# A diffusion trunk's modulation vectors: matmuls with thin weights replaced by row sums on VectorE

## Chip, core and metric

One core of a Trainium2 chip runs the whole program: two layers over 256 context and 256 latent tokens. The metric is device microseconds (us) of one execution; the profile is one further execution.

## What is computed

Each layer derives six modulation vectors of 1024 features from a conditioning vector, once for the latent stream (`c`) and once for the context stream (`c_ctx`):

```python
mod_x = jnp.split((jax.nn.silu(c) @ w_mod[layer] + b_mod[layer])[:, None, :], 6, axis=-1)
mod_c = jnp.split(jax.nn.silu(c_ctx) @ w_mod[layer] + b_mod[layer], 6, axis=-1)
hx = modulate(rms_norm(x, norm_pre_mix[layer]), mod_x[0], mod_x[1])       # shift, scale
x = x + mod_x[2] * rms_norm(mix_x, norm_post_mix[layer])                  # gate
hx = modulate(rms_norm(x, norm_pre_ffn[layer]), mod_x[3], mod_x[4])
x = x + mod_x[5] * rms_norm(channel_mixer(hx), norm_post_ffn[layer])
```

`w_mod[layer]` is 1024 by 6144, 24 MB in f32. The rest of a layer is a token mixer (mLSTM, HGRN2 and differential attention side by side) and a channel mixer: dense SwiGLU in the first layer, top-2 of 8 experts in the second. The second layer's context stream is only needed for its mixer's inputs, so of its modulation the context needs the first two sixths alone.

## The kernel before

Large products are f32 matmuls in three passes: each weight tile of 128x1024 is split into a high part (`whi`, ScalarE, `whl` line 188) and a low part (`wlo`, a VectorE subtraction), and `mm3` (line 196) issues three matmuls per block. Pairs of `whi` and `wlo` live in a ring: three in the pool `wp`, and two more in the pool `hr` during the first half of the dense part. Weights arrive as 1 MB loads by `load` (line 164) in a ring of raw slots, four in `wp` and four more in `hr`; SyncE (SP) issues them all.

The stages follow each other: mixer 0, dense (gate and up, then down), mixer 1, experts. The modulation is computed in pieces spread over them. `first_mods` makes the first two sixths of layer 0 at the very start. All else goes through `mod_piece(l, g, n)` (line 236): a third `g` of `w_mod[l]` (2048 columns) and two of its eight row blocks (`n`), by two 1 MB loads; for each row block four matmuls into the four 32-column strips of the array, with silu(c) as weights (tile `pm`), and an addition into `macc`; after the fourth piece four transposes (`mt`), the bias, and `mod_affine` (line 314), which multiplies by the norm weights into `aff`.

These pieces are generators in a list `work`, and so are projections of the mixers (`fm`, `tm`). `tick(n)` (line 291) advances the list by n units between the steps of a stage, and it starts the first two entries, which issues their loads. Layer 0's last two thirds (`mods(0, 1) + mods(0, 2)`) stand in mixer 0 between projections. Layer 1's twelve pieces (`mo1`, line 1373) stand: two in mixer 0's attention (line 1299), one in the tail of mixer 0 (line 1342), three in the dense part (line 1394), and six in mixer 1 (line 960). In the gate-and-up loop (lines 1391 to 1405) one `tick(1)` follows each of 40 groups; a group is one `whl` and 24 matmuls into the tile `pgu`, and two groups end in one `swiglu_out` (line 1384), a VectorE product into `hh`.

A planner of the framework puts every instruction in an order per engine before the run, from its own model of durations. Only where `strict` is set (mixer 1's end, experts) is program order kept. `row_out` (line 325) writes a feature vector as 4-byte elements to a DRAM tile `gd`, and `row_in` (line 335) reads it back as a row on all 128 partitions.

Of the kernel before, what the change touches and what calls it, by code (L numbers as in the profile page):

```python
# [12 lines left out]
F32 = mybir.dt.float32  # L13
F32R = mybir.dt.float32r
BF16 = mybir.dt.bfloat16
# [3 lines left out]
ALU = mybir.AluOpType  # L19
AX = mybir.AxisListType  # L20

P = 128
D = 1024
# [32 lines left out]
V_L = 16  # L56
V_PM, V_QM, V_PF, V_QF, V_BM, V_GB, V_LB, V_MN, V_HN, V_DN = 0, 8, 16, 24, 32, 80, 81, 85, 87, 89
V_LN = 90
# [51 lines left out]
def kernel(ctx: ExitStack, tc: tile.TileContext, t: dict, out: bass.AP):  # L110
    nc = tc.nc
# [11 lines left out]
    MM, TR = ordered(nc.tensor.matmul), ordered(nc.tensor.transpose)  # L123
    ACT = ordered(nc.scalar.activation)
    TT, TS = ordered(nc.vector.tensor_tensor), ordered(nc.vector.tensor_scalar)
    STT, RED = ordered(nc.vector.scalar_tensor_tensor), ordered(nc.vector.tensor_reduce)
# [7 lines left out]
    sv = cp.tile([P, V_END], F32, name="sv")  # L134
# [7 lines left out]
    modT = [cp.tile([P, 48, 2], F32, name=f"modT{l}") for l in range(2)]  # L142
    aff = [cp.tile([P, 4, KT, 2], F32, name=f"aff{l}") for l in range(2)]
    sc = cp.tile([P, KT, 32], F32, name="sc")
# [4 lines left out]
    def bank(name, dt=F32):  # L149
        return psp.tile([P, 512], dt, tag="b", bufs=8, name=name)  # L150
# [13 lines left out]
    def load(ap, n=2048, halves=False):  # L164
        pool, b = pick("raw", (wp, 4))
        w = pool.tile([P, n], F32, tag="raw", bufs=b, name="raw")
        if halves:
            for a in (slice(0, n // 2), slice(n // 2, n)):
                nc.sync.dma_start(w[:, a], ap[:, a])
        else:  # L170
            nc.sync.dma_start(w[:, :n], ap)
        return w
# [60 lines left out]

    macc = cp.tile([P, 512], F32, name="macc")

    def mod_piece(l, g, n):

        ws = [load(t["w_mod"][l, k * P:(k + 1) * P, g * 2048:(g + 1) * 2048]) for k in (2 * n, 2 * n + 1)]
        yield
        pm = bank("pm")  # L240
        for k in (2 * n, 2 * n + 1):
            for q in range(4):
                MM(pm[32 * q:32 * q + 32, :], sc[:, k, :], ws[k % 2][:, q * 512:(q + 1) * 512],
                   start=(k % 2 == 0), stop=(k % 2 == 1), skip_group_check=True)
            yield
        if n == 0:
            nc.vector.tensor_copy(macc, pm)
            return
        TT(macc, pm, macc, op=ALU.add)
        if n < 3:  # L250
            return
        yield
        pt = bank("mt")
        for b in range(4):
            nc.tensor.transpose(pt[:, b * P:(b + 1) * P], macc[:, b * P:(b + 1) * P], ident)
        q = 16 * g
        b = sv[:, V_L + l * V_LN + V_BM + q:V_L + l * V_LN + V_BM + q + 16].rearrange("p (g b) -> p g b", g=4)
        TT(modT[l][:, q:q + 16, :].rearrange("p (g b) s -> p g b s", g=4),
           pt.rearrange("p (b g s) -> p g b s", b=4, g=4)[:, :, :, 0:2],
           b.unsqueeze(3).to_broadcast([P, 4, 4, 2]), op=ALU.add)  # L260
        for which in ((0,), (1,), (2, 3))[g]:
            mod_affine(l, which)

    def first_mods(c):

# [38 lines left out]
    def add(*gens):  # L304
        work.extend([g, False] for g in gens)
# [2 lines left out]
        while work:  # L308
            tick(1)

    def mods(l, g):
        return [mod_piece(l, g, n) for n in range(4)]

    def mod_affine(l, which):

        j, v = ((1, V_PM), (2, V_QM), (4, V_PF), (5, V_QF))[which]
        src = modT[l][:, 8 * j:8 * j + 8, :]
        v += V_L + l * V_LN
        n = sv[:, v:v + 8].unsqueeze(2).to_broadcast([P, 8, 2])
        if which in (0, 2):  # L320
            STT(aff[l][:, which], src, 1.0, n, op0=ALU.add, op1=ALU.mult)
        else:
            TT(aff[l][:, which], src, n, op=ALU.mult)

    def row_out(src, streams):

# [179 lines left out]
    def mixer(l, X, banks=None):  # L506
# [450 lines left out]
            ACT(mk_[:, j, :], pp, AF.Copy, scale=0.125)  # L957

        lag[0] = 1
        mo = mods(0, 1) + mods(0, 2) if l == 0 else mo1[6:]  # L960
        for g in (fm(None, 1, (0, 512), use_gt), fm(3, 2, (q0, 512), use_mq), fm(4, 2, (0, 512), use_mk)):
            add(g, *mo[0:1])
            mo = mo[1:]
# [61 lines left out]
        for g in ([fm(9 + c, 2, (q0, 512), use_o(2 * c)) for c in range(2)]  # L1025
# [3 lines left out]
            mo = mo[1:]  # L1029
# [25 lines left out]
        for dst, src in ((bT, g0), (thr, g2)):  # L1055
            pt = bank("pt")[:, 0:256].rearrange("p (a b) -> p a b", a=4)
# [7 lines left out]
        for h in range(4):  # L1064
            if h % 2 == 0:

                S = [hx.tile([P, 4, 512], F32, tag=tg, name="S") for tg in ("b8b", "b8c")]
                for s in range(4):
                    a, b = st_rng[s]
# [42 lines left out]
            for d in range(2):  # L1112
# [7 lines left out]
                dst = hs_[:, tr, h * 64:(h + 1) * 64]  # L1120
# [47 lines left out]
        op = ow.enter_context(tc.tile_pool(name=f"ow{l}", bufs=1))  # L1168
# [18 lines left out]
        if l:  # L1187
            first_raws.extend(load(EARLY[n]) for n in range(2))
            g = load_row(gd)
# [105 lines left out]
                    add(out_first(x[1]))  # L1295

        add(*mo)
        if not l:
            add(*mo1[:2])
        qs = {qt[0]: queries(qt[0])}  # L1300
        for tt in qt:
            if tt < 3:
# [19 lines left out]
        with tc.tile_pool(name=f"xw{l}", bufs=1) as xw, tc.tile_pool(name=f"xo{l}", bufs=1) as xo:  # L1322
            more.update(hl=[(xw, 6 if l == 0 else 2)], nhl=0)
            if l == 0:
                xr = {}
                for i in qt:
                    xr[i] = xo.tile([P, D], F32, tag="xr", bufs=4, name="xr")
                    nc.sync.dma_start(xr[i], t["xin"][i * P:(i + 1) * P, :])
                g = gate_in(xo, *gd, nc.sync)
            w_o = [whl(raw_o[n // 2][:, n % 2 * 1024:(n % 2 + 1) * 1024]) for n in range(4)]  # L1330
            py = {}

            def product(i):
                py[i] = bank("py")
                for _ in out_product(i, py[i]):
                    pass

            def post(*tiles):
                return post_steps(xo, [((mix[:, i, 0:512], py[i]), xr[i], g[:, 1 if i < 2 else 0, :], X[:, i, :]) for i in tiles])

            if l == 0:
                add(*mo1[2:3])
            if l == 0:
                with tc.tile_pool(name=f"xp{l}", bufs=1) as pn:
                    banks = tail(product, post, pn, X, (0, 2), 4, 8, lambda: Start((t["w_fg"][0], t["w_fu"][0])))
                more.update(hl=[], nhl=0)
                return banks
            product(2)
            product(3)
            strict[0] = True  # L1350
            steps = [post_steps(xo, [((mix[:, i, 0:512], py[i]), xr[i], g[:, 0, :], X[:, i, :])], i - 1) for i in qt]
            two, three = steps
            f2, f3 = ex.features(2), ex.features(3)
            for _ in two:
                pass
            for _ in range(4):
                next(three)
            next(f2)
            for _ in three:
                pass  # L1360
            next(f2)
            ex.square(2)
            ex.weighed(2, C2)
            ex.scale(2)
            next(f3)
            next(f3)
            ex.square(3)
            ex.weighed(3, C3)
            strict[0] = False
            return ex  # L1370


    mo1 = [g for n in range(3) for g in mods(1, n)]

    def dense(X, banks):
        with ExitStack() as es:
            hp = es.enter_context(tc.tile_pool(name="hp", bufs=1))
# [2 lines left out]
            hh = [slots(F32, f"hh{f}") for f in range(NF)]  # L1380
            with tc.tile_pool(name="hr", bufs=1) as hr:
                more.update(raw=[(hr, 4)], nraw=0, hl=[(hr, 2)], nhl=0)

                def swiglu_out(f, pg, pu):
                    sg = hr.tile([P, 512], F32, tag="sg", bufs=2, name="sg")
                    ACT(sg, pg, AF.Silu)
                    TT(hh[f], pu, sg, op=ALU.mult)

                for j in range(2):
                    swiglu_out(j, banks[j], banks[2 + j])  # L1390
                for c in range(1, NF // 2):
                    wg, wu = load(t["w_fg"][c]), load(t["w_fu"][c])
                    if c == 1:
                        add(*mo1[3:6])
                    for j in range(2):
                        ps = []
                        for w in (wg, wu):
                            a, b = whl(w[:, j * 1024:(j + 1) * 1024])
                            pd = bank("pgu")
                            for k in range(KT):  # L1400
                                kc = slice(k * P, (k + 1) * P)
                                mm3(pd, a[:, kc], b[:, kc], TH[:, k, :], TL[:, k, :], k == 0, k == KT - 1)
                            ps.append(pd)
                            tick(1)
                        swiglu_out(2 * c + j, *ps)
                drain()
# [3 lines left out]
            acc = [[bank("pd") for _ in range(2)] for i in range(4)]  # L1410
# [30 lines left out]
                for i in tiles[0:2 * (tiles[0] // 2)]:  # L1441
                    nc.sync.dma_start(xs[i * P:(i + 1) * P, :], X[:, i, :])

            add(*mo1[6:6])
            with tc.tile_pool(name="xpd", bufs=1) as pn:
                banks = tail(product, post, pn, X, (1, 0), 6, 8,
                             lambda: Start((t["w_fm"][1, 0], t["w_fm"][1, 1]), lambda: slots(F32R, "w_s")))
# [427 lines left out]
def pack(x, c, ctx, c_ctx, w_mod, b_mod, norm_pre_mix, norm_post_mix, norm_pre_ffn, norm_post_ffn,  # L1875
# [37 lines left out]
    rows[0, R_RB:R_RB + 8] = np.asarray(router_b)[0]  # L1913
    d["vecs"], d["rows"] = vecs, rows
    d["w_fm"], d["w_tm"], d["w_gt"] = np.stack(fm), np.stack(tm), np.stack(gt)
    d["w_mod"] = w_mod
    a = w_mod[0].reshape(2, 4, P, 6, 4, 256)[:, :, :, 0:2]
    d["w_m0"] = np.ascontiguousarray(a.transpose(4, 0, 2, 1, 3, 5).reshape(4, 2, P, 2048))
    d["w_out"] = np.stack([_tm(w_out[l]) for l in range(2)])
# [21 lines left out]
```

## Time and profile before

| what | us |
|---|---|
| median of 3 runs | 2217.36 (2217.22 to 2218.29) |
| profiled execution | 2215.78 |
| its span, first to last instruction | 2214.0 |
| mixer 0 | 0 to 499 |
| dense, gate and up | 499 to 733 |
| dense, down, and its tail | 733 to 880 |
| mixer 1 | 880 to 1185 |
| experts | 1185 to 2214 |

PE is TensorE's matmuls, PEld its weight loads, DVE VectorE, ACT ScalarE, POOL GpSimdE, SP the queue that issues the DMAs. A busy PE is not PE at its peak, since matmuls overlap in the records. A row in brackets with an arrow says how long an engine was idle before the instruction and which engine or DMA ended the wait.

### The profile page before, as it was taken

The page shows a single profiled execution, that of the slowest core. Times are in us where ns is not written, and L with a number is a line of the kernel's source. Part 1 is how long each engine was busy: PE and PEld are TensorE (multiplying, and loading weights), DVE is VectorE, ACT ScalarE, POOL GpSimd, SP SyncE. Part 2 cuts the span into 40 slices and gives each one's busy share as a digit, 9 for nine tenths or more (in the row PEclk, how much of TensorE's full clock was granted, in tenths as well). Part 3 has the DMA queues.
Part 4 walks back from the last instruction along what each step waited for, and adds up shares of the span by engine and source line. Part 5 has one row for each costly group of instructions (what it writes and reads, how often), then busy time and mean ns, then how long its engine had stood idle before and what let it go on. Part 6 is the DMA issues. An engine that isn't in the chain of part 4 may idle for free.

```text
span 2214.0 us, 27692 instructions
## 1 busy us (share of the span) xinstructions
PE 2118.2 (96%) x10532; PEld 1680.6 (76%) x10532; DVE 1566.6 (71%) x2145; ACT 1249.5 (56%) x1832; POOL 87.7 (4%) x82
## 2 busy tenths in 40 slices
PE   7998998999999999999987999999999999999997
PEld 4877666787888788777866888877777777777775
DVE  4758657773222346756678998888888888798887
ACT  3632445652222335524557777767777677776765
POOL 1000003010000001000111000000000000000000
PEclk9999999899999999999998999999999999999999
DMA  7430434047221331435437999899998999989992
GB/s 298 151 105 37 134 141 160 5 190 285 77 77 50 123 117 39 171 107 191 76 130 296 371 369 354 305 345 357 347 357 315 357 359 347 350 324 353 355 356 94
DMA packets 81357, 496.82 MB, mean 224 GB/s; under 512 B 17728, under 2 KB 18752, under 8 KB 23104
## 3 DMA queue, kind: packets, MB, share of 16 engines
q1 hardware_dynamic: 81216, 494.97, 60.7%
q8 instruction: 85, 1.39, 0.3%
q14 instruction: 56, 0.46, 0.1%
HBM read 492.81 MB, written 2.13 MB: 224 GB/s over the span
## 4 chain that ended last, share of the span: by engine, by line
PE 32%; DVE 10%; DMA 4%; issue 2%; ACT 2%; DVEq 0%; ACTq 0%
PE pg L117 19%; PE py L117 10%; DVE wlo L117 8%; DMA raw<-w_eu 3%; ACT whi L117 1%; DMA raw<-w_ed 1%; PE ph L1712 1%; PE pcb L117 0%; PE px L117 0%; DVE X L117 0%; DVE qh L1227 0%; DVE mx L1242 0%; DMA X<-w_eu 0%; PE po L117 0%; PE psc L117 0%
## 5 line engine op out<-in xcount | busy, mean ns | idle before, releaser
L117 DVE TENSOR_TENSOR wlo<-raw,whi 128x1024 fp32r<-128x1024 f32 x815 | 959.2, 1224 | 191.8 <-ACT whi L117 179.0
L117 ACT ACTIVATE whi<-raw 128x1024 fp32r<-128x1024 f32 (+1 forms) x820 | 815.4, 1055 | 273.5 <-PE pgu L117 148.8
L117 PE MATMUL pg<-wlo,TH 128*128 128x512 f32 x896 | 363.3, 405 | 5.7 <-DVE wlo L117 2.1
L117 PE MATMUL pg<-whi,TH 128*128 128x512 f32 x896 | 355.6, 397 | 0.8 <-DVE cf L117 0.8
L117 PE MATMUL pg<-whi,TL 128*128 128x512 f32 x896 | 352.1, 393 | 0.0
L117 PE MATMUL py<-whi,hhl 128*128 128x512 f32 x896 | 289.2, 394 | 0.0
L117 PEld LDWEIGHTS pg<-wlo,TH 128*128 128x128 f32 x896 | 168.3, 188 | 63.8 <-DVE wlo L117 30.2
L117 PEld LDWEIGHTS pg<-whi,TH 128*128 128x128 f32 x896 | 168.3, 188 | 40.3 <-DVE cf L117 1.3
L117 PEld LDWEIGHTS py<-whi,hhl 128*128 128x128 f32 x896 | 168.2, 188 | 38.6
L117 PEld LDWEIGHTS pg<-whi,TL 128*128 128x128 f32 x896 | 168.5, 188 | 35.0
L117 PE MATMUL py<-wlo,hhl 128*128 128x512 f32 x448 | 176.5, 394 | 1.1 <-DVE wlo L117 0.8
L117 ACT ACTIVATE hhl<-ph 128x512 fp32r<-128x512 f32 x56 | 33.4, 596 | 168.8 <-PE ph L1712 168.8
L117 PE MATMUL pgu<-TH,whi 128*128 128x512 f32 x320 | 127.2, 397 | 0.0
L117 PE MATMUL pgu<-TL,whi 128*128 128x512 f32 x320 | 126.6, 396 | 0.0
L117 PE MATMUL pgu<-TH,wlo 128*128 128x512 f32 x320 | 126.5, 395 | 0.0
L117 PE MATMUL pp<-TH,whi 128*128 128x512 f32 (+1 forms) x304 | 116.7, 384 | 0.0
L117 PE MATMUL pp<-TL,whi 128*128 128x512 f32 (+1 forms) x304 | 110.9, 365 | 0.0
L117 PE MATMUL pp<-TH,wlo 128*128 128x512 f32 (+1 forms) x304 | 110.6, 364 | 0.0
L117 PEld LDWEIGHTS py<-wlo,hhl 128*128 128x128 f32 x448 | 84.0, 188 | 21.8 <-DVE wlo L117 2.8
L117 PE MATMUL pm<-raw,sc 128*32 128x512 f32 x384 | 62.7, 666 | 16.4 <-DVE ry L117 9.2
L117 DVE TENSOR_TENSOR hhl<-ph,hhl 128x512 fp32r<-128x512 f32 x56 | 38.6, 690 | 51.0 <-ACT hhl L117 50.9
L117 PEld LDWEIGHTS pgu<-TH,whi 128*128 128x128 f32 x320 | 60.1, 188 | 19.2 <-ACT whi L117 3.4
(342 smaller groups left out, 3194.2 us busy)
## 6 DMA issues: line engine op xcount, KB each, us to landing
raw<-w_eg SPq DMA_DIRECT2D x112, 1024.0 KB, 6.7
raw<-w_eu SPq DMA_DIRECT2D x111, 1024.0 KB, 6.3
raw<-w_ed SPq DMA_DIRECT2D x111, 1024.0 KB, 6.7
raw<-w_mod SPq DMA_DIRECT2D x40, 1024.0 KB, 4.9
raw<-w_fm SPq DMA_DIRECT2D x22, 1024.0 KB, 4.9
raw<-w_fg SPq DMA_DIRECT2D x11, 1024.0 KB, 4.9
raw<-w_fu SPq DMA_DIRECT2D x11, 1024.0 KB, 7.0
raw<-w_fd SPq DMA_DIRECT2D x11, 1024.0 KB, 4.8
```

The costliest lines, as they stand in the source:

```text
L117: ins = op(*args, **kw)
L1712: nc.tensor.transpose(ph[:, j, :], sg[:, j * P:(j + 1) * P], ident)
```

## The change

The pieces of layer 1, and the last sixth of layer 0 (features 5120 to 6143), leave TensorE. Their weights are laid out by feature in DRAM (`w_mv`: per layer 24 blocks of 128 partitions by two features' 1024 inputs). silu(c) and silu(c_ctx) are written to DRAM and read back as rows on all partitions (`srow`, 8 KB per partition in the pool `hr`). A new generator `mod_rows` loads one 1 MB block and forms, for each of its two features and each stream needed, one `tensor_tensor_reduce` on VectorE: the product of the weights with the row, summed over 1024 inputs, started from the bias, the sum going into `modT`. All 28 blocks (4 of layer 0, 24 of layer 1) are added to `work` in the dense part's first step. What remains in mixer 0 is `mods(0, 2048, 2048)` as before and four pieces of half the width. Mixer 1 and the tail of mixer 0 have no pieces any more.

```diff
-    def mod_piece(l, g, n):
-        ws = [load(t["w_mod"][l, k * P:(k + 1) * P, g * 2048:(g + 1) * 2048]) for k in (2 * n, 2 * n + 1)]
+    def mod_piece(l, at, m, n):
+        ws = [load(t["w_mod"][l, k * P:(k + 1) * P, at:at + m], m) for k in (2 * n, 2 * n + 1)]
+        c, nb = m // 4, m // 512
...
+    def mod_rows(l, n, srow, junk):
+        w = load(t["w_mv"][l, n])
+        yield
+        for j in range(2):
+            f = 2 * n + j
+            b = V_L + l * V_LN + V_BM + f
+            for s in range(2 if l == 0 or f < 16 else 1):
+                nc.vector.tensor_tensor_reduce(junk, w[:, j * 1024:(j + 1) * 1024], srow[:, s, :], 1.0, sv[:, b:b + 1],
+                                               ALU.mult, ALU.add, modT[l][:, f, s:s + 1])
+        if n % 4 == 3:
+            mod_affine(l, n // 4)
+        yield
...
-        mo = mods(0, 1) + mods(0, 2) if l == 0 else mo1[6:]
+        mo = mods(0, 2048, 2048) + mods(0, 4096, 1024) if l == 0 else []
...
-            add(*mo1[:2])
...
-                add(*mo1[2:3])
...
+                srow = hr.tile([P, 2, D], F32, name="srow")
+                row_in(srow, *row_out(sc, (0, 1)))
+                junk = hr.tile([P, D], BF16, name="junk")
...
-                        add(*mo1[3:6])
+                        add(*[mod_rows(l, n, srow, junk) for l, n in [(0, 20 + i) for i in range(4)] + [(1, i) for i in range(24)]])
```

`mod_affine` now takes one sixth at a time, and only the latent stream where the context is not needed.

## Rows read from the trace of the kernel before

**Rows 1.** The page: busy time, share and instructions of each engine.
```profile
PE 2118.2 (96%) x10532; PEld 1680.6 (76%) x10532; DVE 1566.6 (71%) x2145; ACT 1249.5 (56%) x1832; POOL 87.7 (4%) x82
```

**Rows 2.** Stretches: length, busy PE, PEld, DVE, ACT, POOL; granted clock, DMA share, GB/s.
```profile
240.00:364.00 124.00, 122.91 (x617) 90.13 (x617) 75.02 (x162) 58.15 (x130) 8.26 (x6) 1.00 0.35 117
364.00:443.00 79.00, 67.98 (x362) 49.61 (x361) 61.47 (x144) 47.81 (x129) 15.91 (x12) 0.85 0.21 84
499.00:733.00 234.00, 232.49 (x1019) 181.99 (x1019) 66.46 (x68) 55.48 (x66) 0.00 (x0) 1.00 0.32 117
880.00:1000.00 120.00, 114.26 (x775) 96.10 (x774) 79.57 (x151) 56.05 (x103) 4.72 (x7) 0.99 0.37 129
1000.00:1100.00 100.00, 96.99 (x569) 76.04 (x568) 62.90 (x142) 46.38 (x101) 5.01 (x4) 0.97 0.56 137
1185.00:2214.00 1029.00, 1007.67 (x4455) 802.01 (x4454) 888.30 (x862) 743.10 (x852) 5.59 (x5) 0.99 0.88 334
```

**Rows 3.** The same stretches for tile pm alone: busy PE, PEld, DVE.
```profile
240.00:364.00 124.00, 10.19 (x64) 1.73 (x64) 2.75 (x4) 1.00 0.35 117
364.00:443.00 79.00, 4.92 (x32) 0.80 (x32) 1.34 (x2) 0.85 0.21 84
499.00:733.00 234.00, 6.39 (x48) 0.94 (x48) 2.06 (x3) 1.00 0.32 117
880.00:1000.00 120.00, 7.22 (x48) 1.16 (x48) 2.08 (x3) 0.99 0.37 129
1000.00:1100.00 100.00, 9.23 (x48) 1.55 (x48) 2.01 (x3) 0.97 0.56 137
```

**Rows 4.** Timeline of PE: start, duration, instruction, idle time before it.
```profile
375.88 1.93 PE L117 MATMUL pm<-raw,sc 128*32 128x512 f32 x8 [6.76 <-DMA raw<-w_mod]
...
467.64 1.92 PE L117 MATMUL pm<-raw,sc 128*32 128x512 f32 x16
469.50 1.97 PE L117 MATMUL pt<-ident,xh 128*128 128x128 f32 x16
```

**Rows 5.** Stretch 372 to 382, as in group 2: granted clock behind the wait.
```profile
372.00:382.00 10.00, 6.12 (x25) 3.59 (x26) 6.93 (x18) 4.57 (x13) 3.02 (x3) 0.51 0.97 399
```

**Rows 6.** Timeline of DVE, in mixer 0's attention and in the gate-and-up loop.
```profile
379.08 0.76 DVE L1242 TENSOR_REDUCE mx<-psc 128x1 f32<-128x256 f32 x2 [2.24 <-PE psc L117]
...
552.02 0.69 DVE L117 TENSOR_TENSOR hh<-pgu,sg 128x512 f32<-128x512 f32 x1 [4.17 <-PE pgu L117]
...
563.22 0.69 DVE L117 TENSOR_TENSOR hh<-pgu,sg 128x512 f32<-128x512 f32 x1 [3.58 <-PE pgu L117]
```

**Rows 7.** Tile pgu: duration min/median/max in ns, first and last start.
```profile
L117 PEld LDWEIGHTS pgu<-TH,whi x320: 186/188/188, 499.3 to 730.0; 128*128 128x128 f32 x160
```

**Rows 8.** Groups by shape: count, busy us, mean ns, idle before and what ended it.
```profile
L117 DVE TENSOR_TENSOR wlo<-raw,whi 128x1024 fp32r<-128x1024 f32 x811 | 956.8, 1227 | 191.8 <-ACT whi L117 179.0 <-DMA raw<-w_eu 3.6 <-DMA raw<-w_ed 1.5
L117 DVE SCALAR_TENSOR_TENSOR X<-po_t,ry,X 128x1024 f32<-128x1024 f32 x5 | 6.4, 1282 | 0.1
L117 DVE SCALAR_TENSOR_TENSOR E<-E,dac 128x512 f32<-128x512 f32 x16 | 12.0, 752 | 0.2
L117 ACT ACTIVATION_READ_ACCUMULATOR E<-psc,mx 128x1 f32 x48 | 9.8, 204 | 0.0
```

**Rows 9.** Timelines of DVE and PE at the start of mixer 0's attention: order of work.
```profile
361.74 6.80 DVE L1227 CAST qh<-qh 64x512 fp32r<-64x512 f32 x4
...
370.67 0.74 DVE L1242 TENSOR_REDUCE mx<-psc 128x1 f32<-128x256 f32 x2
...
364.96 0.38 PE L117 MATMUL psc<-dk,ql 64*128 64x256 f32 x2
```

**Rows 10.** Timeline of SP's queue: start, issue time, what is loaded or written.
```profile
331.07 1.00 SPq L329 DMA_DIRECT2D gd<-aff  x2
...
499.58 2.00 SPq L171 DMA_DIRECT2D raw<-w_mod  x4
```

**Rows 11.** The view of DMA issues: count, KB each, median us to landing.
```profile
grow<-gd SPq DMA_DIRECT2D x5, 512.0 KB, 8.2
```

More of the change, by code (lines that the diff above doesn't have):

```diff
@@ L234 @@
     macc = cp.tile([P, 512], F32, name="macc")
-    def mod_piece(l, g, n):
-        ws = [load(t["w_mod"][l, k * P:(k + 1) * P, g * 2048:(g + 1) * 2048]) for k in (2 * n, 2 * n + 1)]
+    def mod_piece(l, at, m, n):
+        ws = [load(t["w_mod"][l, k * P:(k + 1) * P, at:at + m], m) for k in (2 * n, 2 * n + 1)]
+        c, nb = m // 4, m // 512
         yield
-        pm = bank("pm")
+        pm = bank("pm")[:, 0:c]
         for k in (2 * n, 2 * n + 1):
             for q in range(4):
-                MM(pm[32 * q:32 * q + 32, :], sc[:, k, :], ws[k % 2][:, q * 512:(q + 1) * 512],
+                MM(pm[32 * q:32 * q + 32, :], sc[:, k, :], ws[k % 2][:, q * c:(q + 1) * c],
                    start=(k % 2 == 0), stop=(k % 2 == 1), skip_group_check=True)
             yield
+        acc = macc[:, 0:c]
         if n == 0:
-            nc.vector.tensor_copy(macc, pm)
+            nc.vector.tensor_copy(acc, pm)
             return
-        TT(macc, pm, macc, op=ALU.add)
+        TT(acc, pm, acc, op=ALU.add)
         if n < 3:
@@ L253, in mod_piece @@
         pt = bank("mt")
-        for b in range(4):
+        for b in range(nb):
             nc.tensor.transpose(pt[:, b * P:(b + 1) * P], macc[:, b * P:(b + 1) * P], ident)
[L256 to L262, printed above, removed]
+        q = at // P
+        b = sv[:, V_L + l * V_LN + V_BM + q:V_L + l * V_LN + V_BM + q + 4 * nb].rearrange("p (g b) -> p g b", g=4)
+        TT(modT[l][:, q:q + 4 * nb, :].rearrange("p (g b) s -> p g b s", g=4),
+           pt[:, 0:nb * P].rearrange("p (b g s) -> p g b s", b=nb, g=4)[:, :, :, 0:2],
+           b.unsqueeze(3).to_broadcast([P, 4, nb, 2]), op=ALU.add)
+        for j in range(q // 8, (q + 4 * nb) // 8):
+            mod_affine(l, j)
+    def mod_rows(l, n, srow, junk):
[10 more added lines that the diff above has]
+        yield
     def first_mods(c):
@@ L309, in drain, with mods, mod_affine @@
             tick(1)
[L311 to L317, printed above, removed]
+    def mods(l, at, m):
+        return [mod_piece(l, at, m, n) for n in range(4)]
+    def mod_affine(l, j):
+        if j in (0, 3):
+            return
+        which, v = {1: (0, V_PM), 2: (1, V_QM), 4: (2, V_PF), 5: (3, V_QF)}[j]
+        m = 2 if l == 0 or j == 1 else 1
+        src, dst = modT[l][:, 8 * j:8 * j + 8, 0:m], aff[l][:, which, :, 0:m]
         v += V_L + l * V_LN
-        n = sv[:, v:v + 8].unsqueeze(2).to_broadcast([P, 8, 2])
+        n = sv[:, v:v + 8].unsqueeze(2).to_broadcast([P, 8, m])
         if which in (0, 2):
-            STT(aff[l][:, which], src, 1.0, n, op0=ALU.add, op1=ALU.mult)
+            STT(dst, src, 1.0, n, op0=ALU.add, op1=ALU.mult)
         else:
-            TT(aff[l][:, which], src, n, op=ALU.mult)
+            TT(dst, src, n, op=ALU.mult)
     def row_out(src, streams):
@@ L1297, in mixer @@
         add(*mo)
-        if not l:
-            add(*mo1[:2])
         qs = {qt[0]: queries(qt[0])}
@@ L1341, in mixer @@
             if l == 0:
-                add(*mo1[2:3])
-            if l == 0:
                 with tc.tile_pool(name=f"xp{l}", bufs=1) as pn:
@@ L1370, in mixer @@
             return ex
-    mo1 = [g for n in range(3) for g in mods(1, n)]
     def dense(X, banks):
@@ L1442, in post @@
                     nc.sync.dma_start(xs[i * P:(i + 1) * P, :], X[:, i, :])
-            add(*mo1[6:6])
             with tc.tile_pool(name="xpd", bufs=1) as pn:
@@ L1915, in pack @@
     d["w_fm"], d["w_tm"], d["w_gt"] = np.stack(fm), np.stack(tm), np.stack(gt)
-    d["w_mod"] = w_mod
+    d["w_mod"] = w_mod[0:1]
+    d["w_mv"] = np.ascontiguousarray(w_mod.transpose(0, 2, 1).reshape(2, 24, 2, P, D).transpose(0, 1, 3, 2, 4).reshape(2, 24, P, 2 * D))
     a = w_mod[0].reshape(2, 4, P, 6, 4, 256)[:, :, :, 0:2]
```

## The prediction

> **What bounds the kernel now.** I read the busy times first: TensorE is busy 96% of the span [rows 1]. Such a busy time overlaps, so I went on to the stretches [rows 2], where the limit differs. In gate and up (499 to 733) PE is busy 232.5 of 234 us and VectorE 66.5: PE is the limit, VectorE is idle for 167 us. In the attention of mixer 0 (364 to 443) PE is busy 68.0 of 79 at a granted clock of 0.85, so something else sets the pace. In mixer 1 (880 to 1100) PE is busy 211 of 220 and VectorE 142. The experts, 1029 us, hold nothing of the modulation. Then the pieces alone [rows 3]: in the stretches that lose pieces the tile pm takes 10.2, 4.9, 6.4, 7.2 and 9.2 us of PE. The timelines of PE and VectorE around them [rows 4, 6] show where a piece is work on the path and where it fills a gap. The change buys this PE time with VectorE time in the one stretch where VectorE has room. What is to be seen is whether the room lies where the planner puts the work.
>
> **The change part by part.** The sum is made against the profiled execution, 2215.8 us, which is 1.6 below the median of the runs.
>
> *Mixer 0, 240 to 364.* The four pieces for features 4096 to 6143 take 10.2 us of PE [rows 3] and lose half their columns. PE is busy 122.9 of 124 us there [rows 2]. The bounds are 0, if the saved time falls into waits, and 5.1, half of all. I take 3.5, since the fixed part of a matmul stays.
>
> *Attention of mixer 0.* Two pieces go. [...] VectorE sets the pace here, so the gain is what VectorE loses: it waited 2.24 us for the next scores and about 0.8 in two shorter waits [rows 6], and its two additions into macc take 1.34 [rows 3]. That is 4.4. [...]
>
> *Tail of mixer 0.* The piece takes 1.9 us of PE, and the transposes of the next norm follow at once [rows 4]. I take 1.9; 0 is the other end.
>
> *Gate and up.* Three pieces go. Two groups end in one product into hh; undisturbed these lie 11.2 us apart [rows 6], so a group is 5.6 us. From the first matmul at 499.3 [rows 7] to the product at 552.0 four such pairs took 52.7 instead of 44.8. The gain is 7.9, all on the path, between 6.4 (pm alone [rows 3]) and 7.9.
>
> *Mixer 1.* Six pieces go. The three before 1000 take 7.2 us [rows 3]. They are units that the ticks of the HGRN2 levels hand out; without them the same ticks hand out projections earlier, and the last levels run with nothing beside them. I take 2 of 7.2 (0 to 7.2). The three behind take 9.2, and the projections left over are run off at the end of the stretch with PE busy 97 of 100 [rows 2]; there a saved unit shortens the end. I take 7 (4 to 10). Together 9.
>
> The removals sum to 3.5 + 4.4 + 1.9 + 7.9 + 9 = 26.7.
>
> *The rows.* Blocks 20 to 23 of layer 0 and 0 to 7 of layer 1 need two streams, 4 sums each; the other 16 need 2. That is 12 x 4 + 16 x 2 = 80 sums of 128x1024. No such sum is in the trace. The nearest row is the scalar_tensor_tensor of 128x1024 f32 with two SBUF inputs and a pointer scalar, 1.282 us; the plain tensor_tensor is 1.227 [rows 8]. Reading out the sum could be free or, as on ScalarE, an instruction of 0.204 [rows 8]. So p, the price of one, is 1.23 to 1.49; I take 1.28, as the operands are alike. 80 x 1.28 = 102 us fit into the idle 167. [...]
>
> *Where they lie.* One block is due per tick, and a tick comes every 5.6 us. In the first 12 ticks a tick asks of VectorE 4 x 1.28 for sums, 1.23 for the split [rows 8] and half of 0.69 for the product [rows 6]: 6.70, more than 5.6. Later it is 2.56 + 1.58 = 4.1. So it matters whether splits are served ahead of sums. The planner seems to take what is ready in program order: it ran the casts of the second block of queries from 361.7 on, while the first block's scores were done at 365.3 and their maxima, later in the program, came at 370.7 [rows 9]. The sums of tick n precede the split of group n+1 in the program. Five pairs of parts are ready or made at the start (three slots in wp, two in hr), so group 6 is the first to suffer. The sums can start at about 505: hr opens at 499.6, where the loads into it were issued [rows 10], and the rows need some 5 us, as such a read lands 8.2 us behind its issue at the median [rows 11] with other loads beside it. Five blocks, two products and one split later it is 505 + 20p + 2.6 = 533.2; PE needs that split at 499.3 + 5 x 5.6 + 0.5 = 527.8. It is 5.4 late, and seven more groups add 4p + 1.58 - 5.6 = 1.1 each: 13.1 us at group 13, from where it grows no more. In general the delay is 48p - 48.3. Bounds: 0, if the planner puts splits first, and 23.2 at p = 1.49. I take 13.1, because of the row on the order.
>
> *The DMAs that come with it.* Writing silu(c) as 4-byte elements goes to SP's queue. The planner issued the two gate writes of the dense part at 331.1 [rows 10], 400 us ahead of their place in the program, so I expect these writes in the first microseconds, ahead of some weight loads: 0 to 3 us, taken as 0, since the first parts are split well behind their load. Reading the rows back stands on SP at 499.6 ahead of the loads into hr; behind it are the weights of the fifth group, needed 22 us later: 0. If that cover is gone, up to 8.2 [rows 11]. The 28 blocks at 1 MB per 5.6 us, with 2 MB of gate and up weights per 22.4, ask 281 GB/s; the experts draw 334 [rows 2], so the loads keep up: 0.
>
> Sum: 2215.8 - 26.7 + 13.1 = 2202.2, and with the 1.6 **2204 us**.
>
> **The rivals.**
>
> *Splits first.* If the planner's model has blocks land late or gives splits precedence, the sums fill only idle time: 2215.8 - 26.7 + 1.6 = 2191. For it speaks the idle 167 us; against it the order in [rows 9].
>
> *A dear sum* (slower). The mechanism is the same queue on VectorE with another p. The removals are eaten up where 48p - 48.3 = 26.7, at p = 1.56. [...] Against it: no VectorE row with two f32 inputs is that slow. For it: none of these rows writes a sum. [...]
>
> *Fillers were free.* If the pieces in mixers 0 and 1 only filled waits, so that half of 18.8 comes (9.4), while the sums delay the splits: 2215.8 - 7.9 - 9.4 + 13.1 + 1.6 = 2213. For it: at a clock of 0.85 and 0.51 [rows 2, 5] idle PE time exists, and less work could lower the clock further.
>
> **How the numbers follow.** Forecast 0.42 (2198 to 2211), splits first 0.25, fillers free 0.17, a dear sum above 1.56 0.10, and 0.06 for a start or a queue that I don't foresee. A measurement of this kernel can tell about 0.2% from no change, which is 2212.9 to 2221.8. Faster: nearly all of the first two cases and a quarter of the third, 0.68 with a little of the rest. Same: most of the third and the upper part of the forecast's bounds, 0.18. Slower: 0.14. The range for 8 in 10 leaves out the doubled sum and the best end of splits first: 2190 to 2222.
>
> **What would show it.** In the changed trace: sums of 1.2 to 1.5 us, 80 of them, all between 500 and 680; the products into hh 13 to 14 us apart up to about the twelfth tick and 11.2 apart behind it; PE's waits there ended by wlo. In mixer 0's attention no wait of PE for w_mod. Mixer 1 shorter by 9. The forecast is wrong if pgu never waits for wlo (then it is 2191), if a sum is over 1.56, or if mixer 1 keeps its length.

## The result, and the profile after

| | kernel before | changed kernel |
|---|---|---|
| median of 4 runs, us | 2217.64 (2217.22 to 2218.29) | 2194.51 (2190.91 to 2196.47) |
| ratio, 95% interval | | 0.991 (0.9896 to 0.9924) |
| profiled execution, its span | 2215.78, 2214.0 | 2196.47, 2194.7 |

The change takes off 23.1 us by the medians; I had forecast 13.4 (2204). By the ratio with its interval it is 17 to 23 us, and the spans of the two profiled executions differ by 19.3. A second comparison, on the chip of the last experiments, gave 0.9914 (0.9895 to 0.9933).

To see where it went I cut both spans at the first instruction of a stage (first `psc`, first `xr` load, first `pgu`, first `pd`, last `w_s`, first `px`). Lengths in us:

| stage | before | after | difference | forecast |
|---|---|---|---|---|
| mixer 0 up to its attention | 364.2 | 360.8 | -3.4 | -3.5 |
| attention of mixer 0 | 81.2 | 78.9 | -2.3 | -4.4 |
| tail of mixer 0 | 53.9 | 56.6 | +2.7 | -1.9 |
| gate and up | 233.3 | 233.1 | -0.2 | -7.9 + 13.1 |
| down, tail of the dense part | 151.6 | 150.7 | -0.9 | 0 |
| mixer 1 | 297.6 | 280.7 | -16.9 | -9 |
| experts | 1032.2 | 1033.9 | +1.7 | 0 |

The differences add up to those 19.3 us. The experts read 1032.1 to 1034.8 in all the runs below whatever was changed elsewhere, mixer 0 up to its attention 357.9 to 360.8 and the attention 78.7 to 80.9 with the same change in them; differences of that size are not explained one by one here.

The page of the changed kernel, part 1 (compare [rows 1]):

```profile
PE 2085.9 (95%) x10326; PEld 1677.5 (76%) x10326; DVE 1653.8 (75%) x2290; ACT 1248.8 (57%) x1832; POOL 86.7 (4%) x82
```

TensorE (PE) lost 32.3 us of busy time and VectorE (DVE) gained 87.2. Of the 32.3 the span shows 19.3, so some came back as waits. The stretches of the changed kernel that matter (columns as in [rows 2]), gate and up first, then mixer 1 in its early and late part up to the end of its attention:

```profile
496.40:729.40 233.00, 226.69 (x962) 181.54 (x960) 161.74 (x228) 54.48 (x65) 0.00 (x0) 0.99 0.66 221
...
880.00:979.60 99.60, 93.07 (x601) 81.37 (x600) 67.84 (x127) 48.66 (x86) 4.72 (x7) 0.98 0.27 92
979.60:1111.10 131.50, 120.18 (x718) 99.70 (x717) 96.01 (x200) 71.23 (x157) 16.62 (x13) 0.95 0.23 81
```

In gate and up PE is busy for 226.7 of 233.0 us, where before it was busy nearly all the time; the pieces are gone and a hole stands in their place. The groups by shape for that stretch (count, busy us, mean ns, idle time before and what ended it) say what the sums cost:

```profile
L117 PE MATMUL pgu<-TH,whi 128*128 128x512 f32 x320 | 127.8, 399 | 4.8 <-ACT whi L117 4.8
...
L274 DVE CUSTOM_DVE_ANT_0 junk<-raw,srow,sv 128x1024 bf16<-128x1024 f32 x80 | 102.5, 1281 | 5.1 <-DMA srow<-gd 3.5
...
L117 DVE TENSOR_TENSOR wlo<-raw,whi 128x1024 fp32r<-128x1024 f32 x40 | 48.9, 1222 | 31.5 <-ACT whi L117 30.9
...
L274 DVE DVE_READ_ACCUMULATOR2_ANT modT<- 128x1 f32 x80 | 6.6, 83 | 0.0
```

A sum is 1.281 us, the price of the scalar_tensor_tensor of [rows 8], and a read-out of 0.083 us follows it as an instruction of its own; behind one another, sums start 1.33 us apart. And PE's only wait for an operand here is one of 4.8 us for `whi`, ScalarE's high part, not for `wlo`. The place, on PE's timeline and on VectorE's, ScalarE's and SP's:

```profile
563.46 0.39 PE L117 MATMUL pgu<-TH,wlo 128*128 128x512 f32 x1
568.65 0.80 PE L117 MATMUL pgu<-TH,whi 128*128 128x512 f32 x1 [4.81 <-ACT whi L117]
569.25 0.63 PE L117 MATMUL pgu<-TL,whi 128*128 128x512 f32 x1
```

```profile
557.30 0.08 DVE L274 DVE_READ_ACCUMULATOR2_ANT modT<- 128x1 f32 x1
...
562.74 1.28 DVE L274 CUSTOM_DVE_ANT_0 junk<-raw,srow,sv 128x1024 bf16<-128x1024 f32 x1
563.95 0.08 DVE L274 DVE_READ_ACCUMULATOR2_ANT modT<- 128x1 f32 x1
568.64 1.23 DVE L117 TENSOR_TENSOR wlo<-raw,whi 128x1024 fp32r<-128x1024 f32 x1 [4.61 <-ACT whi L117]
```

```profile
567.55 2.95 ACT L117 ACTIVATE whi<-raw 128x1024 fp32r<-128x1024 f32 x3 [8.66 <-DMA raw<-w_fg]
```

```profile
551.62 0.35 SPq L171 DMA_DIRECT2D raw<-w_mv  x1
557.41 0.34 SPq L171 DMA_DIRECT2D raw<-w_fg  x1
```

Read from the bottom up. The load of the next gate weights (`w_fg`) was issued at 557.41, and SP's waits for 552 to 558 name what it waited for:

```profile
SPq L171 <- DVE modT L274: 5.4, 1, 5.4
```

That is 5.4 us for `modT`, a read-out of VectorE. It is the one at 557.30, the last sum of a block that held the raw slot. The weights landed 10 us later, ScalarE split them at 567.55, and PE and VectorE stood still together. Behind the wait PE runs at half clock for a while (the same stretches view):

```profile
563.50:568.60 5.10, 0.35 (x2) 0.00 (x0) 0.53 (x2) 1.05 (x2) 0.00 (x0) 0.81 0.75 296
568.60:573.30 4.70, 4.64 (x11) 3.58 (x12) 4.66 (x7) 1.90 (x3) 0.00 (x0) 0.50 0.01 5
573.30:578.00 4.70, 4.70 (x21) 3.76 (x21) 4.66 (x7) 0.60 (x1) 0.00 (x0) 0.98 0.61 214
```

At 0.50, 11 matmuls pass in 4.7 us, and at 0.98 it is 21. By my estimate from these two counts the half clock costs about 2 us more, and the wait with it about 7 of the 7.9 that the removed pieces gave.

### The profile page after: what moved, and what is told of

It is laid out like the page before. It is cut to its first block, busy times and chain, and to the rows that moved or that the text cites. A ratio compares the mean times of both kernels' runs of the same rounds, so it can differ in the third digit from the quotient of the medians.

```text
span 2194.7 us, 27432 instructions
## 1 busy us (share of the span) xinstructions
PE 2085.9 (95%) x10326; PEld 1677.5 (76%) x10326; DVE 1653.8 (75%) x2290; ACT 1248.8 (57%) x1832; POOL 86.7 (4%) x82
## 4 chain that ended last, share of the span: by engine, by line
PE 36%; DVE 8%; DMA 2%; ACT 2%; issue 2%; DVEq 0%; ACTq 0%
PE pg L117 22%; PE py L117 12%; DVE wlo L117 6%; DMA raw<-w_eu 2%; ACT whi L117 1%; PE ph L1727 1%; PE pcb L117 0%; DVE X L117 0%; PE px L117 0%; DVE qh L1246 0%; DVE mx L1261 0%; PE po L117 0%; DVE tT L117 0%; PE psc L117 0%; ACT sg L117 0%
## 5 line engine op out<-in xcount | busy, mean ns | idle before, releaser
L274 DVE CUSTOM_DVE_ANT_0 junk<-raw,srow,sv 128x1024 bf16<-128x1024 f32 x80 | 102.5, 1281 | 5.1 <-DMA srow<-gd 3.5
```

Of the source, the lines that this page charges most:

```text
L274: nc.vector.tensor_tensor_reduce(junk, w[:, j * 1024:(j + 1) * 1024], srow[:, s, :], 1.0, sv[:, b:b + 1], ALU.mult, ALU.add, modT[l][:, f, ...
```

## The experiments

My theory A after this reading: the twelve heavy blocks (4 sums each) ask VectorE for 16 x 1.33 + 4 x 1.22 + 2 x 0.69 = 27.5 us in four ticks of 5.6, which are 22.4. VectorE falls behind. It doesn't keep the splits waiting, because they take turns with the sums; it keeps the raw slots, and the next gate weights stand in line for them. The rivals are B, the 28 MB of blocks are in the way on the DMA engines, and C, the prediction's, that splits stand behind sums. The planner makes a new order for each kernel, so the runs are compared stage by stage, with the cuts of the table above.

**e1_mixed: heavy and light blocks in turn.**

```diff
-add(*[mod_rows(l, n, srow, junk) for l, n in [(0, 20 + i) for i in range(4)] + [(1, i) for i in range(24)]])
+two = [(0, 20 + i) for i in range(4)] + [(1, i) for i in range(8)]
+one = [(1, i) for i in range(8, 24)]
+mix = [x for pair in zip(two, one) for x in pair] + one[len(two):]
+add(*[mod_rows(l, n, srow, junk) for l, n in mix])
```

> The changed kernel with the blocks in another order: each block of two streams (4 sums) is followed by one of one stream (2 sums), instead of the twelve heavy ones first. Same sums, same 28 MB, same ticks. Theory A (VectorE falls behind while heavy blocks follow each other, a block then keeps its raw slot, the load of the next gate weights waits for that slot, and ACT and PE wait for the weights): four ticks now ask VectorE for 12 x 1.33 + 4 x 1.22 + 2 x 0.69 = 22.2 us in 22.4, nothing piles up, the wait of 4.8 us for whi and the half clock behind it (2 us) go: gate and up 233.0 to 226.5, total 2194.5 to 2188. Theory B (the 28 MB are in the way of the gate weights on the DMA engines): the bytes are the same, a wait for whi of 3 to 6 us stays somewhere, total within 2 us of 2194.5.

Measured: 0.9885 (0.9869 to 0.9901), gate and up 225.8 us, no wait of PE in it above 1.5 us, and that one at its end. This is what A gave, and B's wait is gone with all bytes still loaded.

**e2_own: blocks in slots of their own.**

```diff
-    def mod_rows(l, n, srow, junk):
-        w = load(t["w_mv"][l, n])
+    def mod_rows(l, n, srow, junk, pool):
+        w = pool.tile([P, 2048], F32, tag="raw", bufs=4, name="raw")
+        nc.sync.dma_start(w, t["w_mv"][l, n])
...
-                more.update(raw=[(hr, 4)], nraw=0, hl=[(hr, 2)], nhl=0)
+                more.update(hl=[(hr, 2)], nhl=0)
...
```

> The changed kernel with slots of their own for the modulation's blocks: they take turns in the four slots of the pool of the dense part, the gate and up weights in the four others, so that no weight load waits for a sum. Heavy blocks still first. Theory A (the sums delay the weights only through the shared slots): no wait for whi above 1 us, gate and up 226 to 227.5, total 2188 to 2190. Theory B (the bytes are in the way): the wait of 3 to 6 us stays, 2194. Theory C, the prediction's (splits wait on VectorE behind the sums): the slots don't matter, PE waits for wlo, 2194 or more.

Measured: 0.9882 (0.9864 to 0.9899), gate and up 225.8 us. The waits of PE in this stretch, whole (engine, what it waited with and for, us, times, longest), and the stretch itself:

```profile
PE pd L117 <- ACT h_h L117: 1.5, 1, 1.5
```

```profile
494.70:720.50 225.80, 224.30 (x963) 180.44 (x961) 161.71 (x228) 55.17 (x65) 0.00 (x0) 1.00 0.77 228
```

VectorE is busy for the same 161.7 us as in the changed kernel, the heavy blocks still come first, and PE no longer notices. Against C speaks that nothing waits for `wlo`. The order on VectorE in this kernel shows why:

```profile
541.99 1.28 DVE L275 CUSTOM_DVE_ANT_0 junk<-raw,srow,sv 128x1024 bf16<-128x1024 f32 x1
543.19 0.09 DVE L275 DVE_READ_ACCUMULATOR2_ANT modT<- 128x1 f32 x1
543.19 1.22 DVE L117 TENSOR_TENSOR wlo<-raw,whi 128x1024 fp32r<-128x1024 f32 x1
544.33 1.28 DVE L275 CUSTOM_DVE_ANT_0 junk<-raw,srow,sv 128x1024 bf16<-128x1024 f32 x1
```

A split gets in between two sums of one block: a sum and a split change places one for one, and only the sums run late.

**e3_no_sums: loads without sums.** Each `tensor_tensor_reduce` becomes a `tensor_copy` of one column.

> The changed kernel without the row sums: all 28 blocks are loaded, and each sum is replaced by a copy of one column (128x1), so modT of the last sixth of layer 0 and of layer 1 is not computed. Only the gate-and-up stretch is to be read, since the experts' routing may differ behind it. Theory A: VectorE asks for 70 us there, no slot is held, gate and up 225 to 226 us, no wait of PE above 1 us. Theory B (loads in the way): the wait for whi stays at 3 to 6 us, gate and up 231 to 233.

Measured: gate and up 225.7 us, no wait for `whi`. The loads alone cost nothing: B falls a second time. Taking all 80 sums away gives no more than e1 and e2 gave with all of them in place (225.8).

**e8_own_112: more sums than the kernel needs.** The kernel of e2 with `for s in range(2)` for all blocks.

> The kernel of e2 (slots of their own for the blocks) with two streams in all 28 blocks: 112 sums in place of 80, 42 us more on VectorE. Only the gate-and-up stretch is to be read. Theory A (splits that are ready take turns with sums, and only a shared slot brings VectorE's backlog to PE): VectorE 205 of 226 us busy, sums run later, no wait of PE above 1 us, first pgu to first pd 226 to 228. Theory C (the prediction's: splits stand behind the sums of their tick, 1.1 us per group later as long as a tick asks for 6.8 in 5.6): the delay grows through all 20 groups, 240 or more.

Measured: gate and up 225.8 us once more. In a stretch as long that begins 1.8 us earlier, PE is busy throughout with VectorE busy for 199.8:

```profile
495.00:721.00 226.00, 226.00 (x979) 182.23 (x977) 199.79 (x290) 54.46 (x63) 0.00 (x0) 1.00 0.71 228
```

C is out by more than 14 us. With slots of their own even 32 sums too many are hidden, because a sum that is late keeps nobody waiting before the end of the loop. C's mechanism does show once, in a kernel whose order was changed ahead of this stage (e5 below): there PE waits for `wlo` in gate and up, the longer time for a split that stands behind the first sum, which itself waits 2.1 us for `srow`:

```profile
PE pgu L117 <- DVE wlo L117: 3.7, 2, 2.8
```

**The tail of mixer 0.** It grew by 2.7 us though a piece of 1.9 left it. In the changed kernel PE ends the last product of the output projection (`py`) at 461.6 and waits for `xh`, the rows that the norm has scaled and that PE transposes next (`pt`). The timelines are those of PE, then of VectorE:

```profile
465.00 3.65 PE L117 MATMUL pt<-ident,xh 128*128 128x128 f32 x16 [3.43 <-DVE xh L117]
```

```profile
459.72 0.16 DVE L117 TENSOR_SCALAR rv<-pn_ss 128x2 f32<-128x2 f32 x1
460.57 2.36 DVE L117 TENSOR_TENSOR wlo<-raw,whi 128x1024 fp32r<-128x1024 f32 x2 [0.68 <-ACT whi L117]
462.85 0.15 DVE L117 TENSOR_TENSOR rw<-ry 128x2 f32<-128x2 f32 x1
...
464.10 1.42 DVE L117 TENSOR_SCALAR xh<-X,ry 128x1024 f32<-128x1024 f32 x2
```

Two splits of gate weights stand between the steps of the norm, and one more ahead of them (458.58). In the kernel before those three came at 467.5, 479.1 and 480.7, behind `xh`:

```profile
466.12 1.42 DVE L117 TENSOR_SCALAR xh<-X,ry 128x1024 f32<-128x1024 f32 x2
```

Counted from the first `xr` load `xh` starts at 20.7 us there and at 24.4 in the changed kernel. In the kernel before it was done as the last `py` ended, and PE went from `py` to the piece and on to `pt` without a wait [rows 4]. There two loads for the pieces were issued ahead of these weights, at 448.3, and the weights at 449.4 and 451.7, 4.0 and 6.3 us behind the first `xr` load; now it is 2.9 and 3.4. Two edits of the order and a filler test this.

*e4_norm*: `strict[0]`, which keeps program order, is set around the norm of the first two tiles and the splits of the first group.

> The changed kernel with one order written out in the tail of mixer 0: the steps of the norm of the first two tiles (squares, rstd, scaling) stand in program order ahead of the four splits of the first gate and up weights on ACT and VectorE, where in the changed kernel three splits (3.6 us) came between the sum of squares and xh, PE waited 3.43 us for xh and ran at half clock for the 5 us behind it. Theory D (the tail gave back its gain because the splits, whose weights now land earlier, went ahead of the norm): the wait falls below 1 us, the granted clock stays near 1.00, the tail (last xr load to first pgu) 56.8 to 52, total 2194.5 to 2190. Theory E (the piece that stood there only filled a wait of the norm's chain): PE still waits 2 to 3 us and the clock still falls; total within 1.5 us of 2194.5.

Measured: 0.9911 (0.9896 to 0.9927), tail 58.4. Not what D wanted, but no test of it either: the splits of the second group, outside the ordered part, still got ahead of the norm (two at 459.25), and those inside it then held up a product that frees a bank of PSUM (PE waited 1.2 us for `xh` and 4.0 for `po_t`).

*e5_norm_all*: the ordered part also takes in the two steps of the post norm, ahead of the splits, and the splits of the second group.

> The changed kernel with a longer order written out in the tail of mixer 0: squares, rstd and scaling of the first two tiles, then the squares and products of the last two post norms, and only then the splits of the first two groups of gate and up weights, on ACT and VectorE. Theory D (the tail gave back its gain because splits got ahead of the norm's chain): xh ends about 3 us earlier, PE waits under 1 us before the transposes, the granted clock stays at 1.00 there, the tail (first xr load to first pgu) 56.8 to 52 us, total 2190. Theory E (the piece only filled a wait of the chain itself): the wait stays over 2 us and the clock still falls, tail 55 or more, total 2193 to 2196.

Measured: 0.9924 (0.9905 to 0.9943), tail 58.0. The wait for `xh` is gone, and in its place stand other waits of PE:

```profile
PE pgu L117 <- ACT whi L117: 2.3, 2, 2.1
PE st L117 <- DVE TL L117: 2.1, 2, 1.9
PE st L117 <- DVE wlo L117: 0.9, 1, 0.9
PE st L117 <- ACT whi L117: 0.6, 1, 0.6
```

So D's gain does not come from putting all of the norm first: what is put behind, here four splits in a row, is what PE waits for next (`st` are the products of the first gate and up weights). The order of the kernel before, with the splits one by one behind `xh`, was not written out in any run.

*e9_fill*: the kernel of e2, and the matmuls of one piece back where the kernel before had them, on rows that lie in SBUF.

> The kernel of e2 with the matmuls of one piece (16 products of 128x32 by 512 columns and one addition, on rows that lie in SBUF, no loads) put back into the tail of mixer 0, between the last py and the transposes of the norm, where the kernel before had one. The output does not depend on them. Theory E1 (the piece there was free, and by filling the wait it kept the granted clock up): tail (first xr load to first pgu) 56.2 to 54 us, total 2 us below r_own. Theory E2 (what the tail lost came with the gate weights landing earlier, ahead of which there is no piece's load any more; the filler itself is only in the wait): PE waits 1.5 us in place of 3.4, the clock falls all the same, tail 56 to 56.5. Theory E3 (the piece is work on the path): 58.

Measured beside the kernel of e2 on one chip (r_own, below): tail 56.7 against 56.6, 2187.55 against 2187.57 us. PE in this kernel:

```profile
462.37 1.92 PE L117 MATMUL pm<-TH,sc 128*32 128x512 f32 x16
466.35 1.94 PE L117 MATMUL pt<-ident,xh 128*128 128x128 f32 x16 [2.06 <-DVE xh L117]
```

The stretch 465 to 470 in this kernel and then in r_own:

```profile
465.00:470.00 5.00, 2.58 (x19) 2.17 (x20) 4.47 (x14) 2.76 (x7) 0.73 (x1) 1.00 0.46 193
465.00:470.00 5.00, 5.00 (x26) 4.89 (x25) 4.47 (x8) 4.13 (x10) 1.58 (x2) 0.54 0.23 95
```

The granted clock behind the shorter wait stayed at 1.00, where r_own shows 0.54, and yet the tail is no shorter: the transposes take 1.94 us in place of 3.65, and PE then waits 1.9 us for results of VectorE and GpSimdE in place of 0.6. E1 and E3 fall. Where `xh` is late, neither the piece's work on PE nor the clock sets the length of the tail; the chain through the other engines does, and the piece is free. Whether it was free in the kernel before, where `xh` came in time, this run does not show. E2 is near in the length (56 to 56.5) and wrong in the clock, which it had fall. That the earlier weights are the reason for the 2.7 us is read from the two traces alone: no run put the old times of the loads back. That stays open.

**Mixer 1: what a piece was worth.** The forecast had 9 us, and the change gave 16.9. The whole stage, before and then after:

```profile
884.20:1181.80 297.60, 267.08 (x1648) 214.40 (x1646) 204.01 (x423) 147.27 (x307) 29.98 (x24) 0.95 0.46 141
880.10:1160.80 280.70, 250.15 (x1543) 210.86 (x1542) 198.83 (x412) 147.08 (x307) 29.95 (x24) 0.95 0.30 105
```

PE's busy time fell by 16.9 us too, and its idle time is 30.5 us in both. The pieces alone had taken 7.2 and 9.2 of it [rows 3]. Two runs put one half of each of the six pieces back, the products or the loads.

*e6_products*: at the pieces' places the same 96 matmuls, additions and transposes without their loads.

> The changed kernel with the matmuls of six pieces put back into mixer 1 at the places where the kernel before has them (16 products of 128x32 by 512 columns each, on rows that lie in SBUF, with the additions and transposes), but without their weight loads. The output does not depend on them. Theory F (mixer 1 is paced by PE all along, so that each piece costs its own PE time): from the first load tile of layer 1's projections (last w_s) to the first px 280.7 becomes 295 to 298, nearly all of the 16.9 us that the change took off. Theory G (the prediction's: the early three mostly filled gaps): 9 us or less come back.

Measured: 0.9951 (0.9935 to 0.9967), mixer 1 291.1 us, 10.4 more than the changed kernel. The tile pm in the early and the late part (busy PE, PEld, DVE):

```profile
872.00:980.00 108.00, 7.22 (x48) 1.16 (x48) 2.07 (x3) 1.00 0.25 85
980.00:1110.00 130.00, 6.81 (x48) 1.38 (x48) 2.05 (x3) 0.96 0.24 82
```

*e7_loads*: the 12 loads, each read by one copy, without the products.

> The changed kernel with the 12 loads of 1 MB of those six pieces put back into mixer 1, each read by one copy of a column, without the products. The output does not depend on them. Theory F: 0 to 1.5 us longer from last w_s to first px. Rival H (part of what was gained in mixer 1 is slots and DMA time, the loads of the projections coming earlier without the pieces'): 3 to 8 us longer.

Measured: 0.9926 (0.9901 to 0.995), mixer 1 284.4 us, 3.7 more. The part up to the last `pa` (the products of the HGRN2 levels), in this kernel and in the changed kernel:

```profile
880.10:987.10 107.00, 99.22 (x600) 86.16 (x599) 69.25 (x139) 48.45 (x86) 4.72 (x7) 0.92 0.55 203
880.10:979.60 99.50, 92.97 (x600) 81.27 (x600) 67.74 (x127) 48.66 (x86) 4.72 (x7) 0.98 0.27 92
```

PE passes the same 600 matmuls in both and is busy with them for 6.2 us more, at a lower granted clock; its idle time grew by 1.3. Behind a wait of 3.9 us for `ez`, a product of VectorE, the clock is 0.50 for 934 to 944, where the changed kernel waits 2.9 and shows 0.94. Behind that part mixer 1 is 3.8 us shorter than in the changed kernel (177.4 for 181.2).

The kernels that leave mixer 1 as it is in the changed kernel show 278.7 to 282.3 there, so each of the two figures can be off by 2 us. Products alone bring back 10.4 of 16.9, between F (14 to 17) and G (9 or less) and above what G allowed. Loads alone bring 3.7, which is H's size but not H's mechanism: what grew is PE's time at half clock, and no wait of PE there is for a load. All twelve loads come early in this run (the last copy is at 951), so it doesn't show what they cost in the kernel before. The 2.8 left over are within these errors; in the kernel before the late products took 9.2 us [rows 3], in e6, with no load to wait for, 6.8.

**A version that is faster than both.** One chip, all beside the same kernel before.

> The changed kernel once more, as the base for the three beside it on the same chip: its ratio to the kernel before 0.990 to 0.992, and the wait of PE for whi in gate and up again 3 to 5 us.

> The kernel of e2 (blocks in slots of their own) once more beside the changed kernel: 6 to 8 us below it, all of it in gate and up.

> Slots of their own and heavy and light blocks in turn, both at once. Theory A: either alone already takes the whole stall away, so nothing is left for the second: gate and up 225.8 us again, the total within 2 us of r_own.

| | median us | ratio to the kernel before | gate and up |
|---|---|---|---|
| r_after, the changed kernel | 2196.12 | 0.9914 (0.9895 to 0.9933) | 231.1 |
| r_own, blocks in slots of their own | 2187.57 | 0.9880 (0.9860 to 0.9899) | 225.8 |
| r_own_mixed, and heavy and light in turn | 2185.99 | 0.9871 (0.9851 to 0.9891) | 225.8 |

r_own is 8.6 us below the changed kernel by the medians, a little more than expected; 5.3 of that, and not all of it as expected, is in gate and up, where r_after shows its wait for `whi` again, with 3.6 us. The other 3 are within what medians of these runs differ by. Turning the order as well adds nothing that can be told: the stall was all there was to take.

## Why the prediction was right or wrong

**The sum.** The forecast for the profiled execution was 2202.2 and it took 2196.5. The misses by stage cancel in part: tail +4.6, attention +2.1, gate and up -5.4, mixer 1 -7.9, and the rest +0.9 together (each measured less forecast). That the total came this near is in part luck. By the prediction's own sign, "wrong if pgu never waits for wlo", the step behind the 13.1 failed, and the products into `hh` lie 9.6 to 11.9 us apart but for one gap of 16.8, not 13 to 14.

**Mixer 0 up to the attention**: right, -3.4 for -3.5; with 357.9 to 360.8 in the other runs the agreement to 0.1 is chance. In 240 to 364 the tile pm took 5.92 us with half the columns, where it took 10.19 [rows 3]: a fixed part stayed, as I had supposed.

**Attention of mixer 0**: the wait for `w_mod` that [rows 4] shows is gone, as forecast. The step that failed is that VectorE's waits would go with it: VectorE still waits 4.3 us for scores in this stage, in six waits, as before in five, and PE's transposes (`pt`) and products (`po`) wait for VectorE and ScalarE in its place:

```profile
PE pt L1280 <- DVE mx L117: 4.8, 1, 4.8
PE pt L1166 <- DVE mf L117: 4.4, 1, 4.4
PE po L117 <- ACT pT L117: 3.5, 3, 1.8
```

I took 4.4 from waits that had more than one cause; 2.3 came, and with runs between 78.7 and 80.9 even that is not firm.

**Tail**: wrong in sign. The step that failed is "the transposes of the next norm follow at once", from which I took the 1.9: it reads PE alone and supposes that `xh` comes as early without the piece. It came 3.7 us later, with three splits ahead of it, PE waited 3.4 us, and behind the wait, for 465 to 470, the clock was 0.50. Behind such a late `xh` a piece costs nothing (e9); what moved the splits ahead stays open.

**Gate and up**: the removal of 7.9 was right to 0.5: with the stall gone the stretch is 225.8, 7.5 below 233.3. The price p was right, 1.28 to 1.33. Wrong is the step "the sums of tick n precede the split of group n+1", with which a split would wait for all sums ahead of it. I took that from [rows 9], where a whole group of casts went ahead; here splits and sums take turns, as e2's timeline shows, and e8 rules the formula out, since it has nothing to say on slots. Of the rivals "splits first" was the nearer one, and the backlog of VectorE that the forecast was about did exist; it reached PE by another road, the slots, and cost 7 in place of 13.1. I had the slots in front of me (eight raw slots in one ring for weights and blocks) and costed the loads by rate alone, 281 against 334 GB/s. e3 shows that the loads keep up. What was not asked is when a slot comes free.

On the sum itself: the read-out, which I had as free or 0.204 us as on ScalarE, is an instruction of 0.083 us. The sum has two f32 sources in SBUF and an accumulator, and at 1.281 us for 1024 columns it takes as long as the scalar_tensor_tensor without an accumulator (1.282 [rows 8]). The 80 sums took 1.272 to 1.287 us each; no run shows a sum of twice that price, the doubled sum that the prediction's range leaves out.

**DMAs**: right. The writes of silu(c) were issued at 237.23 and not in the first microseconds, but PE's waits did not grow: from 225 to 300 it has one, of 1.3 us, in both kernels; the rows are read back at 496.57, and VectorE waits 3.5 us for them, which no wait of PE answers to.

**Mixer 1**: the step that failed is "without them the same ticks hand out projections earlier, and the last levels run with nothing beside them", which made 2 of 7.2 out of the early three. The last `pa` of the HGRN2 levels came 105.6 us after the last `w_s` before and 99.5 after (first and last start of the tile, before and then after):

```profile
L117 PE MATMUL pa<-zq,el x336: 270/275/580, 151.9 to 989.8; 128*128 128x128 f32 x168
```

```profile
L117 PE MATMUL pa<-zq,el x336: 270/275/422, 152.0 to 979.6; 128*128 128x128 f32 x168
```

That is 6.1 of 7.2 in the early part, 10.8 behind it, where I had 7 of 9.2. PE's idle time in the early part rose by 1.1 us only, from 5.4 to 6.5. There was other work for the ticks to the end, and over the whole stage the change gave what PE's busy time lost. A price of the pieces' loads apart from that is not shown (e7).

**Rivals**: a dear sum did not occur. What I set against it, that no VectorE row with two f32 inputs is so slow, holds for the rows shown; in the trace of the kernel before one scalar_tensor_tensor of 128x512 (`tT`, near 1178) took 2.908 us, another of that shape 0.742. "Fillers were free" is true of the tail alone, and there only shown for the changed order (e9). As for less work and a lower clock: over the attention it was 0.87 where it had been 0.85, over the tail 0.94 where it had been 1.00.

## What to carry to other kernels

A ring of slots that two streams share ties them to the slower reader (here SP waited 5.4 us for a sum's read-out before it issued the next gate weights): ask for each new load whose release lets it start, not only whether the bandwidth suffices. Work that nobody waits for soon (the sums here: gate and up 225.8 us with 80 or 112 of them in slots of their own, 225.7 with none) costs nothing on an engine with room as long as it holds nothing that others need; buffers of its own took the stall away here, and so did an order that spreads the heavy blocks. And whether a removed piece pays can't be read from one busy engine alone: in the tail of the kernel before PE was busy 98% of the time and taking the piece out gave nothing, as VectorE's next result came later in the new order; in mixer 1 PE was busy 90% and the stage fell by all that PE's busy time lost.

## What the runs showed of the hardware

A VectorE sum of 1024 products per partition from two f32 sources in SBUF, with a bf16 product written beside it, takes 1.281 us, as much as a scalar_tensor_tensor of that shape (1.282); its read-out is a second instruction of 0.083 us, and the pair repeats every 1.33 us. Behind a wait of 4.8 us, and behind one of 3.4 us, PE's granted clock was 0.50 to 0.54 for the next 4.7 to 5 us; behind one of 2.06 us, with 1.92 us of products ahead of it, it stayed at 1.00, and the stage was no shorter (56.7 us for 56.6), because another chain set the time.
